# The last share of an output projection, its norm and the MLP's first tiles by halves of the tokens

## The chip, the cores and the metric

The kernel runs on one core of one Trainium2 chip, in one launch. The metric is the device time of the program in microseconds, the median of several runs. The engines that matter here are TensorE (PE, with its weight load PEld), VectorE (DVE), ScalarE (ACT), and SyncE (SP), which issues most DMAs.

## The reference

Two layers of a hybrid backbone for 512 latent tokens and 256 context tokens of width 1024. Cut to what matters:

```python
for l in range(2):
    need_ctx = l < 1
    hl = modulate(rmsnorm(xl, norm1[l]), ml[:, 0], ml[:, 1])      # latents
    hc = modulate(rmsnorm(xc, norm1[l]), mc[:, 0], mc[:, 1])      # context
    # hl @ w_in, hc @ w_in; three head groups: DeltaNet (256 columns of the output),
    # windowed attention (512), HGRN2 (256); the latents read the context, too
    yl = concatenate([dn_l, sw_l, hg_l], -1) @ w_out[l]           # 512 x 1024
    xl = xl + ml[:, 2] * yl
    h = modulate(rmsnorm(xl, norm2[l]), ml[:, 3], ml[:, 4])
    xl = xl + ml[:, 5] * (square(relu(h @ w_ff1[l])) @ w_ff2[l])  # 1024 -> 4096 -> 1024
    if need_ctx: ...                                              # the same for xc
return rmsnorm(xl, norm_f)
```

`rmsnorm` needs a sum over the 1024 channels of each token, so nothing of `h` for a token exists before all eight column tiles of the projection have been added into `xl` for that token.

## The kernel before

Activations lie with the channels on the partitions: `seg.x[k]` is 128 channels x 512 tokens (256 for the context), k = 0 to 7. Products are made in three matmuls of a high and a low part each (`product_t`, L544): the weights of one column tile come as one piece (`piece`, L534), SP loads it into a stage, ACT casts it into the high part (L540) and VectorE subtracts that to get the low part (L541); then, for each of the 128-row tiles of the input, L554 to L556 issue high x high, high x low and low x high into one PSUM bank. Stages and split weights are rings of two buffers each:

```python
self.st = Ring(self, 2, 1024)
self.ev = Ring(self, 2, 512)
self.wh = Ring(self.wmem, 2, 1024)
self.wl = Ring(self.wmem, 2, 1024)
```

A ring gives its buffers out in the order of the program, so the third user of a ring waits for the first one's readers; `ev` holds the squares, the diagonal and the modulated tiles of the norm. PSUM banks go out the same way, by kind (`bank`, L327): kind "d" (products and, before, the MLP's norm) has banks 0 and 1, "dn" (`product_n`, L560, the first product of a projection) 0, 1, 3, 4, 5, 6, and "n" 4 to 7.

The norm is `rstd` (L617): ACT squares each tile (L627), VectorE adds (L628), PE sums over the partitions with a column of ones (L631), VectorE runs a chain of small instructions (L634, L515 to L520) for the reciprocal root, lays it on a diagonal (L638), and PE spreads it over all partitions (L640). `modulated` (L643) then makes the eight input tiles: VectorE multiplies (L650), ACT adds the shift into the high part (L653), VectorE makes the low part (L654).

`out_proj` (L1464) makes the output projection for some of the eight input tiles ("yd" two, "ys" four, "yh" two), one column tile m after the other, each added into `seg.x[m]` (L1480). In layer 0 the latents' projection takes all eight input tiles at once; the program then has the MLP's norm and operand, then the next layer's projection of the context (`context_in`: four 800-wide pieces of `product_n`, nine products of 256 columns), then the context's own chain with the latents' MLP (L1486) as filling. In layer 1 the projection goes in three shares, "ys", "yh" and, last, "yd", whose pieces are 128 KB; then the two memory regions `r2` and `r3` change their type and the MLP and the final norm follow.

The order of instructions on each engine is set by a planner at build time, which runs the program through a model of its timing. It takes the ready instruction of the highest priority; priority is the order of the program, moved by `high_priority(500)` for everything in `piece` and by `ahead` for whole streams. On the chip each engine then runs its list in that order.

Of the kernel before, what the change touches and what calls it, by code (L numbers as in the profile page):

```python
# [19 lines left out]
DEPTH = 2  # L20
# [152 lines left out]
class Mem:  # L173
# [5 lines left out]
    def __init__(self, tile_ap, n):  # L179
        self.ap, self.n = tile_ap, n  # L180
        self.t = [0] * n
# [27 lines left out]
class Buf:  # L209
# [5 lines left out]
    def free(self):  # L215
        m = self.mem
        Mem.clock += 1
        m.t[self.i:self.i + self.nb] = [Mem.clock] * self.nb
        self.v = None


class Ring:
# [11 lines left out]
    def free(self):  # L234
        for b in self.b:
            b.free()


class Seg:
# [5 lines left out]
class Split:  # L245
# [59 lines left out]
class Net:  # L305
# [225 lines left out]
            yield c  # L531


    def piece(self, src, n=1024):  # L534
        nc = self.nc
        with self.tc.high_priority(500):
            st = self.st(n)
            nc.sync.dma_start(out=st, in_=src)
            hi, lo = self.wh(n), self.wl(n)
            nc.scalar.copy(hi, st)  # L540
            nc.vector.tensor_tensor(out=lo, in0=st, in1=hi.bitcast(F32), op=ALU.subtract)  # L541
        return hi, lo
# [75 lines left out]
    def rstd(self, seg, bk="d"):  # L618

        nc, T, nb = self.nc, seg.T, seg.nb  # L620
        acc = self.get(T, True)
        for k in range(8):
            if k == 0:
                nc.scalar.activation(out=acc.v, in_=seg.x[k], func=AF.Square)
            else:
                q = self.ev(T)
                nc.scalar.activation(out=q, in_=seg.x[k], func=AF.Square)  # L627
                nc.vector.tensor_tensor(out=acc.v, in0=acc.v, in1=q, op=ALU.add)  # L628
        ps = self.bank(bk)
        for b in range(nb):  # L630
            nc.tensor.matmul(ps[:, b:b + 1], lhsT=acc.v[:, b * 128:b * 128 + 128], rhs=self.c["ones"][:, 0:1], start=True, stop=True)  # L631
        acc.free()
        ms = self.small(nb)
        nc.vector.tensor_scalar(out=ms, in0=ps[:, :nb], scalar1=1.0 / D, scalar2=EPS, op0=ALU.mult, op1=ALU.add)  # L634
        rs = self.rsqrt(ms, nb)
        dg = self.ev(T)
        for b in range(nb):
            nc.vector.tensor_scalar(out=dg[:, b * 128:b * 128 + 128], in0=self.ident, scalar1=rs[:, b:b + 1], scalar2=None, op0=ALU.mult)  # L638
        pb = self.bank(bk)[:, :T]
        nc.tensor.matmul(pb, lhsT=self.c["ones"], rhs=dg, start=True, stop=True)  # L640
        return pb

    def modulated(self, l, which, seg, pb=None):  # L643
        nc = self.nc
        if pb is None:
            pb = self.rstd(seg)
        h = self.split(seg)
        for k in range(8):
            t = self.ev(seg.T)
            nc.vector.scalar_tensor_tensor(out=t, in0=seg.x[k], scalar=self.gmul[l][:, which, k, seg.idx:seg.idx + 1], in1=pb,  # L650
                                           op0=ALU.mult, op1=ALU.mult)
            sh = self.mod(l, 3 * which, k, seg)
            nc.scalar.activation(out=h.hi(k), in_=t, func=AF.Identity, bias=sh)  # L653
            nc.vector.scalar_tensor_tensor(out=h.lo(k), in0=t, scalar=sh, in1=h.hi(k).bitcast(F32), op0=ALU.add, op1=ALU.subtract)  # L654
        return h


    def in_piece(self, l, name):
# [802 lines left out]

    Y_TILES = {"yd": (0, 1), "ys": (2, 3, 4, 5), "yh": (6, 7)}

    def out_proj(self, l, seg, names=("yd", "ys", "yh"), mems=None):  # L1464

        nc, r = self.nc, seg.r
        ks = [k for n in names for k in self.Y_TILES[n]]
        y = [r[n][i] if n == "ys" else r[n][:, i] for n in names for i in range(len(self.Y_TILES[n]))]
        h = Split(mems or self.split_mems(), seg, len(ks))
        for k in range(len(ks)):  # L1470
            nc.scalar.copy(h.hi(k), y[k])
            nc.vector.tensor_tensor(out=h.lo(k), in0=y[k], in1=h.hi(k).bitcast(F32), op=ALU.subtract)
        for n in names:
            for b in ("sq0", "sq1") if n == "ys" else (n,):
                seg.b[b].free()
        if seg.x is None:
            self.x_load(seg)
        for m in range(8):
            def evac(seg, ps):
                nc.vector.scalar_tensor_tensor(out=seg.x[m], in0=ps, scalar=self.mod(l, 2, m, seg), in1=seg.x[m], op0=ALU.mult, op1=ALU.add)  # L1480
            yield from self.product_t(self.io["wout"][l, m][:, ks[0] * 128:(ks[-1] + 1) * 128], [(seg, h)], evac, len(ks))
        h.free()

    def mlp(self, l, seg):
        nc = self.nc
        h = self.modulated(l, 1, seg)  # L1486
        yield 0.0
        f = self.split(seg)
        for g in range(4):
            for k in range(8):  # L1490
                def evac(seg, ps):
                    t = self.ev(seg.T)
                    nc.scalar.activation(out=t, in_=ps, func=AF.Relu)  # L1493
                    nc.scalar.activation(out=t, in_=t, func=AF.Square)  # L1494
                    nc.scalar.copy(f.hi(k), t)  # L1495
                    nc.vector.tensor_tensor(out=f.lo(k), in0=t, in1=f.hi(k).bitcast(F32), op=ALU.subtract)  # L1496
                yield from self.product_t(self.io["ff1"][l, g * 8 + k], [(seg, h)], evac)
# [22 lines left out]
    def run(self, stop=None):  # L1520
        self.setup()
        lat, ctx = self.lat, self.ctx
# [58 lines left out]
        self.region_type(F32R, "r2", "r3")  # L1581
        run(bg.rest())
        self.project(1, (ctx,))
        run(self.out_proj(0, lat))
        mlp = self.mlp(0, lat)
        next(mlp)
        run(context_in())
        Ub = self.delta_open((ctx,))
# [46 lines left out]
        Ub.free()  # L1635
        self.region_type(F32R, "r1")
        run(self.out_proj(1, lat, ("yh",)))
        run(self.out_proj(1, lat, ("yd",)))
        self.region_type(F32R, "r2", "r3")
        run(self.mlp(1, lat))  # L1640
        self.finish()
        for n in ("r1", "r3", "r2"):
# [27 lines left out]
```

## Time and profile before

| | us |
|---|---|
| median of 3 runs | 2105.99 (2104.21 to 2106.32) |
| profiled execution, its own time | 2100.87 |
| its span | 2099.0 |
| PE, DVE, ACT busy | 1972.9, 1216.8, 858.1 |
| mean granted TensorE clock | 0.966 of full |

The span is what lies between the first and the last instruction of the profiled execution; busy times are sums of instruction durations and overlap. TensorE's clock has two levels, 1.0 and 0.5 of full speed in the rows. A matmul's row shows its whole passage, so the pace of a dense stretch is read from the starts of its rows, not from their durations.

### The profile page before, as it was taken

To read this page: it belongs to the slowest core of one execution; us is meant where nothing else is said; L and a number is where in the kernel's file an instruction comes from. 1 tells how busy PE (TensorE), PEld (TensorE's weight loads), DVE (VectorE), ACT (ScalarE), POOL (GpSimd) and SP (SyncE) were. 2 spreads that over 40 slices of the span, in tenths; PEclk is the share of its full clock that TensorE was granted. 3 is DMA by queue.
4 is the path that set the end of the run, shared out by engine and by line. 5 is a ranking of instruction groups with operands and counts; after the bars stand their busy time and mean duration, and the time that the engine had idled before them with its cause. 6 is when DMAs were issued, how large, how long until landed. Compare 5 with 4: busy or idle time off the path is not lost.

```text
span 2099.0 us, 37907 instructions
## 1 busy us (share of the span) xinstructions
PE 1972.9 (94%) x15456; PEld 1622.8 (77%) x15456; DVE 1216.8 (58%) x2737; ACT 858.1 (41%) x1703; POOL 143.7 (7%) x281
## 2 busy tenths in 40 slices
PE   5999999999999998799999998999889979999996
PEld 2787889879899997788788876767678747888884
DVE  4574883856976676766333334757787573333334
ACT  2432353335556663552524332425644234334241
POOL 0001333000000000011000000011200000000000
PEclk9999997999999999899999998999999989999998
DMA  8435343164232342333222246363300222222221
GB/s 341 155 111 166 99 121 112 42 237 152 100 112 102 102 160 72 129 127 119 81 91 100 90 151 192 114 208 121 111 2 13 72 70 101 91 101 91 100 91 70
DMA packets 72445, 242.43 MB, mean 115 GB/s; under 512 B 10192, under 2 KB 12368, under 8 KB 72144
## 3 DMA queue, kind: packets, MB, share of 16 engines
q1 hardware_dynamic: 57456, 197.35, 27.9%
q0 software_dynamic: 11792, 34.14, 5.1%
q10 hardware_dynamic: 3024, 8.53, 1.2%
q8 instruction: 121, 1.98, 0.4%
q14 instruction: 52, 0.43, 0.1%
HBM read 218.21 MB, written 19.14 MB: 113 GB/s over the span
## 4 chain that ended last, share of the span: by engine, by line
PE 80%; DVE 7%; DMA 5%; issue 4%; ACT 2%; POOL 1%; ACTq 0%; DVEq 0%; POOLq 0%; SPq 0%
PE psum L554 20%; PE psum L556 20%; PE psum L555 20%; PE psum L590 2%; PE psum L1452 2%; PE psum L1443 2%; PE psum L1390 1%; DMA arena<-in_ada 1%; PE psum L1117 1%; DVE weights L541 1%; PE psum L1075 1%; PE psum L1079 1%; DMA r<-in_ada 1%; DVE arena L1273 1%; DVE arena L1280 1%
## 5 line engine op out<-in xcount | busy, mean ns | idle before, releaser
L554 PE MATMUL psum<-r,weights 128*128 128x512 f32 (+1 forms) x2304 | 829.9, 361 | 11.0 <-ACT arena L725 3.8
L556 PE MATMUL psum<-r,weights 128*128 128x512 f32 (+1 forms) x2304 | 826.2, 360 | 2.1 <-DVE weights L541 2.0
L555 PE MATMUL psum<-r,weights 128*128 128x512 f32 (+1 forms) x2304 | 824.8, 358 | 0.4 <-DVE r L654 0.2
L540 ACT CAST weights<-arena 128x1024 fp32r<-128x1024 f32 (+3 forms) x295 | 293.7, 996 | 689.5 <-PE psum L555 601.2
L541 DVE TENSOR_TENSOR weights<-arena,weights 128x1024 fp32r<-128x1024 f32 (+3 forms) x295 | 340.8, 1156 | 298.0 <-ACT weights L540 289.4
L554 PEld LDWEIGHTS psum<-r,weights 128*128 128x128 f32 x2304 | 435.6, 189 | 95.5 <-issue 11.1
L556 PEld LDWEIGHTS psum<-r,weights 128*128 128x128 f32 x2304 | 435.6, 189 | 73.8 <-DVE weights L541 6.1
L555 PEld LDWEIGHTS psum<-r,weights 128*128 128x128 f32 x2304 | 435.9, 189 | 68.5 <-issue 3.0
L1500 DVE SCALAR_TENSOR_TENSOR arena<-psum,arena 128x512 f32<-128x512 f32 (+1 forms) x96 | 63.4, 661 | 196.8 <-PE psum L556 196.5
L1496 DVE TENSOR_TENSOR r<-arena,r 128x512 fp32r<-128x512 f32 (+1 forms) x96 | 57.4, 601 | 38.0 <-ACT r L1495 37.7
L653 ACT ACTIVATE r<-arena 128x512 fp32r<-128x512 f32 (+1 forms) x56 | 33.1, 628 | 71.3 <-DVE arena L650 71.3
L590 PE MATMUL psum<-arena 128*32 128x256 f32 x576 | 51.4, 406 | 9.3 <-DMA arena<-in_ada 8.7
L1494 ACT ACTIVATE arena<-arena 128x512 f32<-128x512 f32 (+1 forms) x96 | 54.1, 564 | 2.4
L1495 ACT CAST r<-arena 128x512 fp32r<-128x512 f32 (+1 forms) x96 | 52.8, 553 | 2.4
L1390 PE MATMUL psum<-r 128*128 128x256 f32 (+1 forms) x256 | 52.7, 321 | 0.5 <-ACT r L1423 0.5
L1493 ACT ACTIVATE arena<-psum 128x512 f32<-128x512 f32 (+1 forms) x96 | 50.2, 523 | 0.0
L1480 DVE SCALAR_TENSOR_TENSOR arena<-psum,arena 128x512 f32<-128x512 f32 (+1 forms) x40 | 27.7, 696 | 35.1 <-PE psum L556 34.8
L572 PE MATMUL psum<-weights,r 128*128 128x400 f32 x96 | 35.0, 378 | 10.7 <-DVE arena L650 10.1
L590 PE MATMUL psum<-r,arena 128*32 128x256 f32 x192 | 23.1, 497 | 19.2 <-DMA r<-in_ada 19.2
L1452 PE MATMUL psum<-arena 128*64 128x128 f32 x456 | 38.7, 294 | 2.2 <-ACT arena L1436 2.2
L650 DVE SCALAR_TENSOR_TENSOR arena<-arena,psum 128x512 f32<-128x512 f32 (+1 forms) x56 | 33.0, 628 | 12.9 <-PE psum L640 12.8
L1448 ACT COPY arena<-psum 128x512 f32<-128x512 f32 x53 | 31.1, 589 | 22.2 <-PE psum L1443 20.8
(426 smaller groups left out, 2573.5 us busy)
## 6 DMA issues: line engine op xcount, KB each, us to landing
arena<-in_ff SPq DMA_DIRECT2D x192, 512.0 KB, 3.2
arena<-in_ada SPq DMA_DIRECT2D x72, 512.0 KB, 4.9
arena<-in_win SPq DMA_DIRECT2D x51, 512.0 KB, 3.9
r<-in_ada SPq DMA_DIRECT2D x24, 512.0 KB, 5.4
arena<-in_wout SPq DMA_DIRECT2D x16, 512.0 KB, 3.6
arena<-in_win SPq DMA_DIRECT2D x12, 400.0 KB, 3.7
arena<-in_x ACTq DMA_DIRECT2D x8, 512.0 KB, 7.0
arena<-arena POOLq DMA_DIRECT2D x40, 64.0 KB, 4.6
```

The lines of the kernel that those rows point to most:

```text
L540: nc.scalar.copy(hi, st)
L541: nc.vector.tensor_tensor(out=lo, in0=st, in1=hi.bitcast(F32), op=ALU.subtract)
L554: nc.tensor.matmul(o, lhsT=hi[:, w], rhs=h.hi(k), start=k == 0, stop=False)
L555: nc.tensor.matmul(o, lhsT=hi[:, w], rhs=h.lo(k), start=False, stop=False)
L556: nc.tensor.matmul(o, lhsT=lo[:, w], rhs=h.hi(k), start=False, stop=k == nk - 1)
L590: nc.tensor.matmul(ps[32 * j:32 * j + 32, f * 256:f * 256 + 256], lhsT=self.csil[:, k, :], rhs=st[:, j * 256:j * 256 + 256], start=k == 0, ...
L1390: nc.tensor.matmul(o, lhsT=qs[:, kv], rhs=ks[:, kv, a, c0:c1], start=a == 0, stop=a == 1 and not more)
L1452: nc.tensor.matmul(py[heads[kv]], lhsT=self.vS[:, blocks[k0 + kt], heads[kv]], rhs=PT[:, c:c + 128], start=k0 + kt == 0, stop=k0 + kt == n ...
L1494: nc.scalar.activation(out=t, in_=t, func=AF.Square)
L1495: nc.scalar.copy(f.hi(k), t)
L1496: nc.vector.tensor_tensor(out=f.lo(k), in0=t, in1=f.hi(k).bitcast(F32), op=ALU.subtract)
L1500: nc.vector.scalar_tensor_tensor(out=seg.x[m], in0=ps, scalar=self.mod(l, 5, m, seg), in1=seg.x[m], op0=ALU.mult, op1=ALU.add)
```

## The change

The last share of the latents' output projection (layer 0: "yh", split off from the rest; layer 1: "yd") loads its weights as two pieces of four column tiles each and goes over the tokens in two halves of 256: for each half all eight column tiles, with the squares and their sum beside them, then that half's norm (its two banks now of kind "n"). Then both halves are modulated. In layer 1 the first two column tiles of the MLP go together, by halves. Other products are as before.

```diff
-    def piece(self, src, n=1024):
+    def piece(self, src, n=1024, parts=1):
...
-            nc.sync.dma_start(out=st, in_=src)
+            nc.sync.dma_start(out=st.rearrange("p (m c) -> p m c", m=parts) if parts > 1 else st, in_=src)
...
+    def token_rstd(self, acc, T, bk):       # the norm from the sum of squares on, for T tokens
...
+    def modulate(self, l, which, seg, h, ts, pb):   # the three instructions per k, on tokens ts
...
-    def out_proj(self, l, seg, names=("yd", "ys", "yh"), mems=None):
+    def out_proj(self, l, seg, names=("yd", "ys", "yh"), mems=None, last=None):
...
+        if last:
+            yield from self.last_share(l, seg, h, ks, last)
+            return
...
+    HALVES = slice(0, 256), slice(256, 512)
+
+    def last_share(self, l, seg, h, ks, mem_types):
+
+        nc = self.nc
+        w4 = [self.piece(self.io["wout"][l, m0:m0 + 4, :, ks[0] * 128:(ks[-1] + 1) * 128].rearrange("m p c -> p m c"), 1024, 4) for m0 in (0, 4)]
+        mem_types()
+        acc = self.get(512, True)
+        pbs = []
+        for ts in self.HALVES:
+            for m in range(8):
+                hi, lo = w4[m // 4]
+                o = self.bank("d")[:, :256]
+                for k in range(2):
+                    w = slice(m % 4 * 256 + k * 128, m % 4 * 256 + k * 128 + 128)
+                    nc.tensor.matmul(o, lhsT=hi[:, w], rhs=h.hi(k)[:, ts], start=k == 0, stop=False)
+                    nc.tensor.matmul(o, lhsT=hi[:, w], rhs=h.lo(k)[:, ts], start=False, stop=False)
+                    nc.tensor.matmul(o, lhsT=lo[:, w], rhs=h.hi(k)[:, ts], start=False, stop=k == 1)
+                x = seg.x[m][:, ts]
+                nc.vector.scalar_tensor_tensor(out=x, in0=o, scalar=self.mod(l, 2, m, seg), in1=x, op0=ALU.mult, op1=ALU.add)
+                q = self.ev(256) if m else acc.v[:, ts]
+                nc.scalar.activation(out=q, in_=x, func=AF.Square)
+                if m:
+                    nc.vector.tensor_tensor(out=acc.v[:, ts], in0=acc.v[:, ts], in1=q, op=ALU.add)
+            pbs.append(self.token_rstd(acc.v[:, ts], 256, "n"))
+            yield 8.0
+        acc.free()
+        seg.hm = self.split(seg)
+        for ts, pb in zip(self.HALVES, pbs):
+            self.modulate(l, 1, seg, seg.hm, ts, pb)
+        h.free()
+
+    def first_pair(self, l, seg, h, evacs):
+
+        nc = self.nc
+        ws = [self.piece(self.io["ff1"][l, k]) for k in range(2)]
+        os = [self.bank("d") for _ in ws]
+        for ts in self.HALVES:
+            for k in range(8):
+                w = slice(k * 128, k * 128 + 128)
+                for (hi, lo), o in zip(ws, os):
+                    nc.tensor.matmul(o[:, ts], lhsT=hi[:, w], rhs=h.hi(k)[:, ts], start=k == 0, stop=False)
+                    nc.tensor.matmul(o[:, ts], lhsT=lo[:, w], rhs=h.hi(k)[:, ts], start=False, stop=False)
+                    nc.tensor.matmul(o[:, ts], lhsT=hi[:, w], rhs=h.lo(k)[:, ts], start=False, stop=k == 7)
+        for o, evac in zip(os, evacs):
+            evac(seg, o)
+        yield 10.0
...
     def mlp(self, l, seg):
-        h = self.modulated(l, 1, seg)
+        pair = seg is self.lat and l == DEPTH - 1
+        h = seg.hm if seg is self.lat else self.modulated(l, 1, seg)
...
+            first = pair and g == 0
+            if first:
+                yield from self.first_pair(l, seg, h, [squared(0), squared(1)])
+            for k in range(2 if first else 0, 8):
+                yield from self.product_t(self.io["ff1"][l, g * 8 + k], [(seg, h)], squared(k))
...
-        run(self.out_proj(0, lat))
+        run(self.out_proj(0, lat, ("yd", "ys")))
+        run(self.out_proj(0, lat, ("yh",), None, lambda: None))
...
-        run(self.out_proj(1, lat, ("yd",)))
-        self.region_type(F32R, "r2", "r3")
+        run(self.out_proj(1, lat, ("yd",), [self.region["r1"][1]], lambda: self.region_type(F32R, "r2", "r3")))
```

## Rows read from the trace of the kernel before

**Rows 1.** The page, part 4: the chain that ended last, by engine.

```profile
PE 80%; DVE 7%; DMA 5%; issue 4%; ACT 2%; POOL 1%; ACTq 0%; DVEq 0%; POOLq 0%; SPq 0%
```

**Rows 2.** Waits of PE, whole run: us in total, times, longest us.

```profile
PE psum L631 <- DVE arena L628: 14.8, 6, 3.9
```

**Rows 3.** Windows: span, us, engines' busy (instructions), PEclk, DMA share, GB/s.

```profile
826.40:858.80 32.40, 15.76 (x58) 13.76 (x58) 20.11 (x42) 10.51 (x16) 0.53 (x1) 0.74 0.15 46
1691.50:1705.00 13.50, 12.52 (x48) 8.07 (x48) 11.64 (x21) 6.64 (x14) 0.00 (x0) 1.00 0.30 100
1705.00:1717.40 12.40, 3.10 (x10) 1.47 (x10) 8.56 (x24) 3.50 (x6) 0.00 (x0) 0.68 0.38 126
1717.40:1733.80 16.40, 14.99 (x48) 10.15 (x48) 10.00 (x15) 6.20 (x10) 0.00 (x0) 0.82 0.00 0
```

**Rows 4.** Timeline of PE, layer 0: start us, us, instruction [idle before <-releaser].

```profile
821.97 0.40 PE L554 MATMUL psum<-r,weights 128*128 128x512 f32 x1
...
825.91 0.39 PE L556 MATMUL psum<-r,weights 128*128 128x512 f32 x1
...
846.36 0.70 PE L572 MATMUL psum<-weights,r 128*128 128x400 f32 x1 [10.08 <-DVE arena L650]
...
858.84 0.38 PE L554 MATMUL psum<-r,weights 128*128 128x256 f32 x1 [3.83 <-ACT arena L725]
```

**Rows 5.** Timeline of PE, layer 1.

```profile
1704.60 0.39 PE L556 MATMUL psum<-r,weights 128*128 128x512 f32 x1
...
1717.42 0.80 PE L554 MATMUL psum<-r,weights 128*128 128x512 f32 x1 [1.65 <-ACT r L653]
...
1732.79 0.40 PE L556 MATMUL psum<-r,weights 128*128 128x512 f32 x1
...
1734.69 0.50 PE L556 MATMUL psum<-r,weights 128*128 128x512 f32 x1
```

**Rows 6.** Timeline of PE, products of the context, 256 columns.

```profile
499.80 0.28 PE L555 MATMUL psum<-r,weights 128*128 128x256 f32 x1
...
504.84 0.28 PE L555 MATMUL psum<-r,weights 128*128 128x256 f32 x1
...
860.27 0.41 PE L554 MATMUL psum<-r,weights 128*128 128x256 f32 x1
...
860.91 0.41 PE L554 MATMUL psum<-r,weights 128*128 128x256 f32 x1
```

**Rows 7.** Timeline of DVE, both layers (x2: two merged).

```profile
801.43 0.87 DVE L650 SCALAR_TENSOR_TENSOR arena<-arena,psum 128x256 f32<-128x256 f32 x2
...
1710.34 0.15 DVE L634 TENSOR_SCALAR arena<-psum 128x4 f32<-128x4 f32 x1
...
1712.71 0.87 DVE L638 TENSOR_SCALAR arena<-arena 128x128 f32<-128x128 f32 x4
1715.82 1.41 DVE L650 SCALAR_TENSOR_TENSOR arena<-arena,psum 128x512 f32<-128x512 f32 x2 [2.23 <-PE psum L640]
...
1725.99 1.42 DVE L654 SCALAR_TENSOR_TENSOR r<-arena,r 128x512 fp32r<-128x512 f32 x2
```

**Rows 8.** Groups by line and shape: count | busy us, mean ns | idle before.

```profile
L541 DVE TENSOR_TENSOR weights<-arena,weights 128x1024 fp32r<-128x1024 f32 x259 | 316.8, 1224 | 284.2 <-ACT weights L540 275.8 <-PE psum L1443 1.3 <-PE psum L555 0.3
...
L628 DVE TENSOR_TENSOR arena<-arena 128x256 f32<-128x256 f32 x21 | 8.8, 421 | 3.4 <-ACT arena L627 2.8
...
L540 ACT CAST weights<-arena 128x1024 fp32r<-128x1024 f32 x259 | 272.0, 1051 | 627.8 <-PE psum L555 573.9 <-issue 11.5 <-DMA arena<-in_win 10.8
```

**Rows 9.** DMA issues: count, KB each, median us from issue to landing.

```profile
arena<-in_wout SPq DMA_DIRECT2D x16, 512.0 KB, 3.6
...
r<-hi_lat POOLq DMA_DIRECT2D x1, 512.0 KB, 4.4
```

**Rows 10.** Timeline of SP, layer 1.

```profile
1688.55 0.33 SPq L538 DMA_DIRECT2D arena<-in_wout  x1
```

**Rows 11.** Chain that ended last, layer 0: start us, us, what.

```profile
850.72 5.01 DMA arena<-in_win
```

More of the change, by code (lines that the diff above doesn't have):

```diff
@@ L236, in free, with __init__, hi, lo @@
             b.free()
+class Part:
+    def __init__(self, h, ts):
+        self.h, self.ts = h, ts
+    def hi(self, k):
+        return self.h.hi(k)[:, self.ts]
+    def lo(self, k):
+        return self.h.lo(k)[:, self.ts]
 class Seg:
@@ L628, in rstd @@
                 nc.vector.tensor_tensor(out=acc.v, in0=acc.v, in1=q, op=ALU.add)
+        pb = self.token_rstd(acc.v, T, bk)
+        acc.free()
+        return pb
+    def token_rstd(self, acc, T, bk):
+        nc, nb = self.nc, T // 128
         ps = self.bank(bk)
         for b in range(nb):
-            nc.tensor.matmul(ps[:, b:b + 1], lhsT=acc.v[:, b * 128:b * 128 + 128], rhs=self.c["ones"][:, 0:1], start=True, stop=True)
-        acc.free()
+            nc.tensor.matmul(ps[:, b:b + 1], lhsT=acc[:, b * 128:b * 128 + 128], rhs=self.c["ones"][:, 0:1], start=True, stop=True)
         ms = self.small(nb)
@@ L647, in modulated @@
         h = self.split(seg)
+        self.modulate(l, which, seg, h, slice(0, seg.T), pb)
+        return h
+    def modulate(self, l, which, seg, h, ts, pb):
+        nc = self.nc
+        h = Part(h, ts)
         for k in range(8):
-            t = self.ev(seg.T)
-            nc.vector.scalar_tensor_tensor(out=t, in0=seg.x[k], scalar=self.gmul[l][:, which, k, seg.idx:seg.idx + 1], in1=pb,
+            t = self.ev(ts.stop - ts.start)
+            nc.vector.scalar_tensor_tensor(out=t, in0=seg.x[k][:, ts], scalar=self.gmul[l][:, which, k, seg.idx:seg.idx + 1], in1=pb,
                                            op0=ALU.mult, op1=ALU.mult)
@@ L654, in modulated @@
             nc.vector.scalar_tensor_tensor(out=h.lo(k), in0=t, scalar=sh, in1=h.hi(k).bitcast(F32), op0=ALU.add, op1=ALU.subtract)
-        return h
     def in_piece(self, l, name):
@@ L1482, in out_proj @@
         h.free()
+    HALVES = slice(0, 256), slice(256, 512)
[22 more added lines that the diff above has]
+            yield 8.0
+        acc.free()
+        seg.hm = self.split(seg)
+        for ts, pb in zip(self.HALVES, pbs):
+            self.modulate(l, 1, seg, seg.hm, ts, pb)
+        h.free()
@@ new lines, in first_pair @@
+    def first_pair(self, l, seg, h, evacs):
+        nc = self.nc
+        ws = [self.piece(self.io["ff1"][l, k]) for k in range(2)]
[10 more added lines that the diff above has]
+        yield 10.0
@@ L1489, in mlp, with squared @@
         for g in range(4):
-            for k in range(8):
+            def squared(k):
                 def evac(seg, ps):
@@ L1496, in evac @@
                     nc.vector.tensor_tensor(out=f.lo(k), in0=t, in1=f.hi(k).bitcast(F32), op=ALU.subtract)
-                yield from self.product_t(self.io["ff1"][l, g * 8 + k], [(seg, h)], evac)
+                return evac
+            first = pair and g == 0
[3 more added lines that the diff above has]
+                yield from self.product_t(self.io["ff1"][l, g * 8 + k], [(seg, h)], squared(k))
             for m in range(8):
```

## The prediction

> **What bounds the kernel now.** I read the page first, then the waits of PE, the stages by windows, the engines' timelines around the two places of the change, and the DMA rows. The chain that ended last is 80% matmul [rows 1], so time comes out of the whole only where TensorE stands still or runs at its low clock. The waits of PE over the whole run name the places: the norm's first matmul (L631, behind the sum of squares) [rows 2] and one wait of 10.1 us behind the modulation, L650 [rows 4]. The windows show what these cost around the change [rows 3]. In layer 0, from 826.4 to 858.8 us, PE is busy 15.8 of 32.4 us and the granted clock is 0.74. In layer 1, from 1705.0 to 1717.4, it is busy 3.1 of 12.4 us, and in the next 16.4 us, which hold the first two column tiles of the MLP, the clock is 0.82.
>
> Layer 0 in detail [rows 4]: the latents' output projection issues its last matmul at 825.91; the next layer's context projection follows in the program. Of its first product (four pieces, 48 matmuls of 400 columns) only the half for one token block runs on the first two pieces, and then PE stands until 846.36. Counting the calls of `bank`, the norm's broadcast lies in bank 1 (kind "d") and so does the second token block of that product (kind "dn"); the bank comes free only when the modulation has read the broadcast for the last time. Matmuls of the next products start at 858.84, 32.9 us after the projection's last. Layer 1 in detail [rows 5]: last matmul at 1704.60, first of the MLP 1717.42, the two tiles end with the one at 1732.79, and the third tile runs freely from 1734.69.
>
> **Prices.** A 512-column matmul takes 0.232 us at the full clock (17 steps from 821.97 to 825.91, rows 4). A 256-column one takes 0.120 us (42 steps from 499.80 to 504.84) and 0.21 us at the low clock (three steps from 860.27 to 860.91) [rows 6]. So a halved product costs 2 x 0.120 - 0.232 = 0.008 us more per pair: three places of 48 pairs, 1.2 us, and TensorE does not mind the halves. VectorE does: two modulation steps of 256 columns take 0.87 us, two of 512 take 1.41, so the pace is 0.39 against 0.67 [rows 7] and a cut instruction costs about 0.12 us more. An eviction I price like a modulation step, an add of squares at 0.34 (0.42 less an overlap of 0.08). Splitting a weight piece takes a cast of 1.05 us and a subtraction of 1.22 [rows 8]. The small chain of the norm runs from 1710.34 to 1712.71, 2.4 us, and each 128-column diagonal block 0.22 (0.87 for four): 2.8 us for a half [rows 7].
>
> **Layer 0, step by step.** (1) The first call now carries six of the eight input tiles: 48 matmuls of 512 fewer, 11.1 us, so it ends at about 815.0 instead of 826.1. Its 384 KB pieces are smaller than those before, hidden as they were. (2) The last share is 96 matmuls of 256, 11.5 us on PE. VectorE has in it 16 evictions (6.3), 14 adds (4.8), the subtraction of the second weight block (1.2), that of a context piece (1.0), and the whole chain of the first half (2.8): 16.1 us. VectorE is the longer one, and with two banks PE follows it: last add at about 832, 3 to 4 us later than before. (3) The broadcasts now lie in kind "n", banks 7 and 5 by the count of calls, and the context product in banks 0 and 1: the 10.1 us wait goes. What is late next is the supply of pieces. Two stages hold all pieces, and a transfer starts when the subtraction before it has emptied one: 5.0 us for the transfer [rows 11], then cast and subtraction, a round of 7.3. The rings of split weights are held by the two blocks of the share until its fourth and eighth tile of the second half, so the first context pieces are ready at about 829 and 832, the third and fourth a round later (839), and the fifth and sixth land at 841 to 844.5. The eviction of the 48 matmuls on ACT stands behind the casts that wait for these, as it does now. So the next products begin at about 846 instead of 858.84: 13 us. (4) VectorE has at 832 still the second chain, 32 modulation steps (12.6) and five subtractions (5.5): busy to about 853, and the convolutions of the context's first products queue behind. I take 2 us for it. Layer 0: 11 us less. Bounds: 16 if VectorE's 16.1 us ran at PE's 11.5; 4 if the products could go on only with VectorE free. The MLP's operand is then ready before 860 and first needed at about 875: hidden, and no cost.
>
> **Layer 1, step by step.** (1) The eight 128 KB pieces become two of 512 KB in 1 KB rows. SP's queue is as before up to there: the first is issued at 1688.55 [rows 10], when the ring of stages allows. No row shows this shape on this queue; the nearest are the 512 KB pieces of the same matrix in 4 KB rows (3.6) and a load of 512 KB in 1 KB rows by POOL (4.4) [rows 9], with 5.0 as the far end [rows 11]. I take 4.2, near the second because of the rows: landed 1692.8, split 1695.0. The ends are 1694.4 and 1695.8. PE, done with the share before at about 1691.4, waits 3 us here that it does not wait now. (2) From 1695.0 VectorE has one block's subtraction (1.2), 16 evictions (6.3), 14 adds (4.8), two chains (5.6), the subtractions of the MLP's first two pieces (2.4), and 32 modulation steps (12.6): 32.9 us. Without a hole it ends at 1727.9; now it ends at 1727.41 [rows 7]. The hole: `ev` has two buffers in the program's order, so the first half's second modulation step writes where the second half's diagonal lies until the second broadcast has read it. The early half can then use the wait of the late half through one buffer only. I take 1 us of holes: 1729. (3) The gain is behind that: now 24 matmuls of the second tile are left after the last modulation, since its bank held the broadcast; then six small ones are. PE has 96 matmuls of 256 from about 1717; at first at the low clock, as now to 1723 (26 at 0.21), then 70 at 0.120: 13.9 us, done at 1730 to 1731 against 1733.0. The third tile's wait for its weights and bank stays. Layer 1: 3 us less. Bounds: 6 less with the early landing and no hole; 4.5 more if all 96 run at the low clock (20.4 us from 1717).
>
> **Sum.** 11 + 3 = 14 us off the profiled execution's 2100.87 (span 2099.0 and 1.9 around it): 2086.9. The median of the runs is 5.1 us above that execution, and I carry the difference over: 2105.99 - 14 = 2092.
>
> [...]
>
> **Rivals.** *VectorE's queue takes layer 0 too* (0.20). The modulation of both halves stands ahead of the context's work and the products wait for it. For it: 16.1 us against 11.5 in the share, and 21 us of VectorE work from 832 on. Against: pieces have priority, and ACT, not VectorE, evicts the context's tiles. Layer 0 gains 6, layer 1 nothing: 2100.
>
> *VectorE starves TensorE and the clock goes with it* (0.12). Place: the last share of either layer and the pair of tiles. Where PE works 11.5 of 17 us the granted clock may fall to its lower level, as in the idle stretches [rows 3]. Price at the low clock: a share takes 96 x 0.213 = 20.4 us, 3 to 4 more than VectorE's, the pair the same: layer 1 ends at about 1742, 9 later; in layer 0 the pieces follow 4 us later and their 48 matmuls take 16 us instead of 9, which leaves 3 of the gain. Together 6 slower: 2112. It decides once the share takes more than about 19 us. Against it: in layer 1 the share before ran at clock 1.00 with PE busy 12.5 of 13.5 us.
>
> *Both waits go whole* (0.13). The planner fills VectorE's order well, so that the products begin at 842 and the pair ends at 1727: 17 + 6, 2083.
>
> *The gain is handed back* (0.05). The context's chain, which the latents' MLP only fills, ends when it did, and layer 1 stays: 2105.
>
> **How the numbers follow.** The forecast has 0.50, with a range of its own from 2087 to 2097. The range of 8 in 10 goes from 2083 (the third rival) to 2105 (the fourth); the slower case lies beyond. What this measurement can tell from no change is 0.2%, 4.2 us: faster is below 2101.8, which takes in the forecast, the third rival and two thirds of the first (0.13): 0.76. Within 0.2%: the rest of the first, the fourth, a little of the second: 0.13. Slower: 0.11.
>
> **What would show it.** Layer 0: no wait of L572 behind the modulation; the first product of 256 columns after the share at about 846; VectorE busy over 0.9 in the share and its last add near 832. Layer 1: the first block's transfer 3.6 to 5.0 us; a hole in PE of about 3 us before the share; the last modulation at 1727 to 1730 and the pair's end less than 2 us behind it, in that trace's time less layer 0's gain. I am wrong if the share takes PE's 11.5 us rather than VectorE's 16, if the clock in it is below 0.9, or if the products after it begin later than 852.

## The result and the profile after

The changed kernel is slower: 2117.48 us (median of 4 runs, 2116.32 to 2121.33) against 2106.15 for the kernel before beside it (4 runs), a ratio of 1.0061 with a 95% interval of [1.0044, 1.0079]. The forecast was 14 us faster; it is 11 us slower. The profiled execution took 2121.33 us, its span is 2119.5, the mean granted clock 0.959. Up to 480 us PE's instructions and their order are the same in both kernels, and yet the two profiled executions are already 3.4 us apart there. So below each place is measured from a mark beside it, not from the start of the span.

In the code after, the products are L567 to L569, the share L1526 to L1528 (eviction L1530, squares L1532, adds L1534), the ones matmul L651, the chain L653 and L528 to L533, the diagonal L657, the broadcast L659, the modulation L675, L678 and L679, the pair L1552 to L1554, and the evacuation (the copy out of PSUM) of the context product's v and i columns L749 (L725 before).

Waits of PE, whole run. Of before, [rows 2] shows the ones matmul's; the broadcast's was

```profile
PE psum L640 <- DVE arena L638: 10.6, 4, 4.3
```

After:

```profile
PE psum L659 <- DVE arena L657: 15.5, 6, 4.7
PE psum L651 <- DVE arena L641: 9.4, 4, 3.9
PE psum L651 <- DVE arena L1534: 7.9, 2, 4.3
PE psum L937 <- DVE arena L675: 6.1, 1, 6.1
PE psum L567 <- ACT arena L749: 5.1, 1, 5.1
```

The 10.1 us behind the bank [rows 4] are gone, as forecast. In their place stand waits for the second half's adds (L1534), more for the diagonals, and waits for the modulation (L675) and for an evacuation on ACT (L749). Windows (columns as in [rows 3]): layer 0's share and what follows it; layer 1's share, the rest of the norm, the pair of tiles.

```profile
817.60:831.90 14.30, 13.44 (x102) 12.38 (x100) 13.06 (x35) 6.93 (x14) 0.00 (x0) 1.00 0.23 67
831.90:868.70 36.80, 15.77 (x80) 14.40 (x80) 27.91 (x81) 17.48 (x36) 0.00 (x0) 0.65 0.22 72
1706.80:1723.00 16.20, 14.96 (x100) 13.61 (x100) 13.86 (x35) 6.57 (x14) 0.00 (x0) 0.89 0.23 75
1723.00:1735.50 12.50, 4.64 (x15) 3.08 (x14) 8.26 (x29) 3.63 (x7) 0.00 (x0) 0.67 0.22 80
1735.50:1752.10 16.60, 13.78 (x91) 13.03 (x90) 13.12 (x31) 8.42 (x18) 0.00 (x0) 0.83 0.00 1
```

VectorE does not slow layer 0's share so far that the clock falls: it is busy 13.06 of 14.3 us there, and the clock is 1.00. What is new is the long stretch behind it, in which PE is busy 15.8 of 36.8 us. PE's timeline there (of before: [rows 4]):

```profile
831.61 0.28 PE L1528 MATMUL psum<-r,weights 128*128 128x256 f32 x1
836.29 0.59 PE L659 MATMUL psum<-arena 128*128 128x256 f32 x2
845.61 1.01 PE L651 MATMUL psum<-arena 128*128 128x1 f32 x4 [4.34 <-DVE arena L1534]
851.28 1.19 PE L659 MATMUL psum<-arena 128*128 128x256 f32 x2 [4.66 <-DVE arena L657]
858.60 0.61 PE L937 MATMUL psum<-arena 128*64 128x16 f32 x8 [6.12 <-DVE arena L675]
868.72 0.58 PE L567 MATMUL psum<-r,weights 128*128 128x256 f32 x1 [5.12 <-ACT arena L749]
```

and ACT's, around the evacuation that PE waited for:

```profile
867.90 0.51 ACT L678 ACTIVATE r<-arena 128x256 fp32r<-128x256 f32 x1 [0.40 <-DVE arena L675]
868.32 0.35 ACT L749 COPY arena<-psum 128x256 f32<-128x256 f32 x1
```

The next products begin 37.1 us after the share's last matmul; before it was 32.9. Two things are seen. The second half's sum is ready only at 845.61, 14 us after its last matmul, though its evictions were done. And the v and i columns of the context product, whose last matmul starts at 840.92, are evacuated at 868.32, right behind the last modulated tile.

Layer 1, PE after (of before: [rows 5]):

```profile
1706.86 0.58 PE L1526 MATMUL psum<-r,weights 128*128 128x256 f32 x1 [2.05 <-ACT weights L553]
...
1725.85 0.67 PE L659 MATMUL psum<-arena 128*128 128x256 f32 x2 [2.76 <-DVE arena L657]
1730.07 1.01 PE L651 MATMUL psum<-arena 128*128 128x1 f32 x4 [3.54 <-DVE arena L1534]
1734.29 1.22 PE L659 MATMUL psum<-arena 128*128 128x256 f32 x2 [1.45 <-DVE arena L657]
1736.62 0.58 PE L1552 MATMUL psum<-r,weights 128*128 128x256 f32 x1 [1.12 <-ACT r L678]
1752.15 0.51 PE L567 MATMUL psum<-r,weights 128*128 128x512 f32 x1 [1.52 <-ACT arena L1569]
```

VectorE after, in the same place (of before: [rows 7]):

```profile
1725.23 0.48 DVE L657 TENSOR_SCALAR arena<-arena 128x128 f32<-128x128 f32 x2
1727.01 3.00 DVE L1534 TENSOR_TENSOR arena<-arena 128x256 f32<-128x256 f32 x6 [1.30 <-ACT arena L1532]
1730.11 0.48 DVE L675 SCALAR_TENSOR_TENSOR arena<-arena,psum 128x256 f32<-128x256 f32 x1
...
1735.55 0.87 DVE L675 SCALAR_TENSOR_TENSOR arena<-arena,psum 128x256 f32<-128x256 f32 x2 [1.32 <-PE psum L659]
1736.60 0.89 DVE L679 SCALAR_TENSOR_TENSOR r<-arena,r 128x256 fp32r<-128x256 f32 x2 [0.18 <-ACT r L678]
...
1749.59 0.48 DVE L679 SCALAR_TENSOR_TENSOR r<-arena,r 128x256 fp32r<-128x256 f32 x1 [0.58 <-ACT r L678]
```

Six of the second half's seven adds run in one block right after the first half's broadcast, and all but one of the sixteen modulated tiles after the second half's broadcast. The halves do not overlap: they run one behind the other. The prediction's sum for VectorE began when it had split the first weight block (here 1708.07) and ended with the last modulation (1750.07):

```profile
1708.07:1750.07 42.00, 31.60 (x199) 28.43 (x198) 33.53 (x93) 16.81 (x35) 0.00 (x0) 0.81 0.15 51
```

The work is as forecast, 33.5 us against 32.9, but it takes 42.0: 8.5 us of holes where the sum had 1. In e1 below, which has the same layer 1, it is 33.53 of 41.9 us.

The stretch from the last matmul of the share before to the third MLP tile splits so (us, from the starts of PE's rows in each kernel's one profiled execution; the rest is from there to the end of the span; e1 to e14 are the experiments below):

| | before | after | e1 | e8 | e9 | e4 | e10 | e13 | e14 |
|---|---|---|---|---|---|---|---|---|---|
| to the share's last matmul | 13.8 | 18.4 | 18.2 | 18.5 | 16.1 | 21.4 | 15.3 | 20.4 | 18.8 |
| to the last broadcast | 9.1 | 11.5 | 11.5 | 11.6 | 10.2 | 14.2 | 13.0 | 11.2 | 10.9 |
| to the third tile | 20.2 | 17.9 | 17.9 | 22.8 | 17.9 | 13.4 | 13.3 | 11.6 | 12.0 |
| whole stretch | 43.2 | 47.7 | 47.6 | 52.8 | 44.1 | 49.0 | 41.6 | 43.2 | 41.6 |
| the rest | 365.1 | 367.4 | 367.5 | 367.5 | 368.9 | 367.4 | 367.5 | 369.4 | 367.4 |

So layer 1 loses 4.5 us in the stretch and 2.3 us behind it. One execution can be some us off in the stretch: e3, whose layer 1 is the changed kernel's, has 49.4, and the experiments whose layer 1 is that of before have 42.3 to 42.8.

### The profile page after: what moved, and what is told of

Read it like the earlier page. It is cut to its first block, busy times and chain, and to the rows that moved or that the text cites. A ratio compares the mean times of both kernels' runs of the same rounds, so it can differ in the third digit from the quotient of the medians.

```text
span 2119.5 us, 38314 instructions
## 1 busy us (share of the span) xinstructions
PE 1986.5 (94%) x15604; PEld 1640.5 (77%) x15604; DVE 1232.5 (58%) x2827; ACT 864.8 (41%) x1731; POOL 144.2 (7%) x281
## 4 chain that ended last, share of the span: by engine, by line
PE 82%; DVE 9%; DMA 5%; ACT 2%; issue 2%; POOL 0%; ACTq 0%; DVEq 0%; POOLq 0%
PE psum L567 20%; PE psum L569 20%; PE psum L568 20%; PE psum L603 2%; PE psum L1476 2%; PE psum L1467 2%; PE psum L1414 2%; DMA arena<-in_ada 1%; PE psum L1141 1%; PE psum L1099 1%; PE psum L1103 1%; DVE weights L554 1%; DMA r<-in_ada 1%; DVE arena L1297 1%; DVE arena L1304 1%
## 5 line engine op out<-in xcount | busy, mean ns | idle before, releaser
L567 PE MATMUL psum<-r,weights 128*128 128x512 f32 (+1 forms) x2256 | 810.4, 360 | 9.1 <-ACT arena L749 5.1
L569 PE MATMUL psum<-r,weights 128*128 128x512 f32 (+1 forms) x2256 | 808.3, 359 | 0.9 <-DVE weights L554 0.8
L568 PE MATMUL psum<-r,weights 128*128 128x512 f32 (+1 forms) x2256 | 805.1, 357 | 0.1
L553 ACT CAST weights<-arena 128x1024 fp32r<-128x1024 f32 (+4 forms) x291 | 292.6, 1006 | 691.1 <-PE psum L568 597.4
L554 DVE TENSOR_TENSOR weights<-arena,weights 128x1024 fp32r<-128x1024 f32 (+4 forms) x291 | 340.1, 1169 | 298.3 <-ACT weights L553 289.6
L567 PEld LDWEIGHTS psum<-r,weights 128*128 128x128 f32 x2256 | 426.9, 189 | 89.2 <-issue 11.4
L569 PEld LDWEIGHTS psum<-r,weights 128*128 128x128 f32 x2256 | 426.2, 189 | 70.5 <-DVE weights L554 4.0
L568 PEld LDWEIGHTS psum<-r,weights 128*128 128x128 f32 x2256 | 426.5, 189 | 65.8 <-issue 2.4
L1582 DVE SCALAR_TENSOR_TENSOR arena<-psum,arena 128x512 f32<-128x512 f32 (+1 forms) x96 | 63.4, 661 | 202.4 <-PE psum L569 202.0
L678 ACT ACTIVATE r<-arena 128x256 fp32r<-128x256 f32 (+1 forms) x72 | 37.4, 552 | 74.6 <-DVE arena L675 74.5
L603 PE MATMUL psum<-arena 128*32 128x256 f32 x576 | 51.6, 415 | 11.1 <-DMA arena<-in_ada 10.6
L1571 ACT CAST r<-arena 128x512 fp32r<-128x512 f32 (+1 forms) x96 | 52.8, 553 | 2.4
L675 DVE SCALAR_TENSOR_TENSOR arena<-arena,psum 128x256 f32<-128x256 f32 (+1 forms) x72 | 36.3, 535 | 13.6 <-PE psum L659 13.2
L603 PE MATMUL psum<-r,arena 128*32 128x256 f32 x192 | 23.5, 503 | 20.4 <-DMA r<-in_ada 20.4
L1414 PEld LDWEIGHTS psum<-r 128*128 128x128 f32 x256 | 39.1, 204 | 3.1 <-ACT r L1447 1.6
L679 DVE SCALAR_TENSOR_TENSOR r<-arena,r 128x256 fp32r<-128x256 f32 (+1 forms) x72 | 36.8, 541 | 6.7 <-ACT r L678 5.8
L1476 PE MATMUL psum<-arena 128*64 128x128 f32 x456 | 37.1, 291 | 3.6 <-ACT arena L1460 3.6
```

The lines of the kernel that those rows point to most:

```text
L567: nc.tensor.matmul(o, lhsT=hi[:, w], rhs=h.hi(k), start=k == 0, stop=False)
L568: nc.tensor.matmul(o, lhsT=hi[:, w], rhs=h.lo(k), start=False, stop=False)
L569: nc.tensor.matmul(o, lhsT=lo[:, w], rhs=h.hi(k), start=False, stop=k == nk - 1)
L603: nc.tensor.matmul(ps[32 * j:32 * j + 32, f * 256:f * 256 + 256], lhsT=self.csil[:, k, :], rhs=st[:, j * 256:j * 256 + 256], start=k == 0, ...
L1414: nc.tensor.matmul(o, lhsT=qs[:, kv], rhs=ks[:, kv, a, c0:c1], start=a == 0, stop=a == 1 and not more)
L1476: nc.tensor.matmul(py[heads[kv]], lhsT=self.vS[:, blocks[k0 + kt], heads[kv]], rhs=PT[:, c:c + 128], start=k0 + kt == 0, stop=k0 + kt == n ...
```

## The experiments

Each kernel was timed against the kernel before on the same chip; the ratio is to that kernel. The chips differ between experiments, so ratios are compared, not microseconds.

**Each layer alone (e1, e2).** e1 keeps the old code in layer 0, e2 in layer 1:

```
-        run(self.out_proj(0, lat, ("yd", "ys")))
-        run(self.out_proj(0, lat, ("yh",), None, lambda: None))
+        run(self.out_proj(0, lat))                          # e1
...
-        run(self.out_proj(1, lat, ("yd",), [self.region["r1"][1]], ...))
+        run(self.out_proj(1, lat, ("yd",)))                 # e2, and pair = False
```

> Layer 0 as in the kernel before, layer 1 as in the changed one. Ring theory (the norm's two buffers, given out in the program's order, hold the second half's squares behind the first half's broadcast and the modulation behind the second one's): the layer-1 stretch from the end of the share before to the third MLP tile is 47.5 us as in the changed kernel against 42.5, so +5 us on the kernel before: 2111. Rival (VectorE's extra instructions only: 31 at 0.12 us and one more chain of 2.4): +6, 2112, with VectorE without holes between the share and the last modulation. If layer 0 alone carries the loss: 2106.

> Layer 0 as in the changed kernel, layer 1 as in the kernel before. The traces have the context products starting later by 5 to 6 us in layer 0, so both theories say 2111 to 2113; if the loss comes from layer 1 alone 2106, and 2117 if it all lies here.

e1: 2112.69 us, 1.0036 [1.0022, 1.0050]. e2: 2108.00, 1.0013 [1.0000, 1.0026]. That is 7.6 and 2.7 us; together 0.49% of the 0.61%, within the intervals. Neither layer has the forecast gain. For e1 the two theories lie too close to be told apart by time; the rival asked for a VectorE without holes, and there are 8.4 us of them. e2 lost less than the 5 to 7 us expected.

**The two work tiles (e3, e4).** `ev` has two buffers, given out in the order of the program: squares of the first half, its diagonal, squares of the second half, its diagonal, modulated tiles, then the evacuated v and i columns. e3 gives the latter two buffers of their own; e4 gives the whole last share (squares, diagonals, modulation) a ring of eight.

```
# e3
+        vt = Ring(self, 2, 256) if l == 1 and segs[0] is self.ctx else self.ev
-            t = self.ev(256)
+            t = vt(256)
# e4
+        ev, self.ev = self.ev, Ring(self, 8, 256)           # around last_share
```

> The changed kernel; only the two tiles that take the context product's last 256 columns get buffers of their own instead of the norm's ring. Ring theory: their copies on ACT no longer stand behind the last modulation, the wait of 5 us in front of the first 256-column product goes with the 20 us of idle PE before it, that product starts near 847 instead of 868.7 in the trace's time, and the run comes to 2098 (2094 to 2104). Rival (VectorE is full with the modulation of halves and nothing else can move): the first product moves by less than 5 us and the run stays within 4 us of the changed kernel, 2114 to 2118. Layer 1 is the same by either.

> The changed kernel; the last share, its norm and its modulation use a ring of eight buffers of 256 columns of their own in both layers, the old ring is left to the rest. Ring theory: layer 0 as with the tiles' own buffers (20 us less) and in layer 1 the second half's squares follow their evictions and the first half's modulation starts before the second broadcast: 6 to 9 us less there, together 2090 (2085 to 2098). Rival (VectorE full): layer 1 gains under 2 us, 2098 if layer 0 moves, 2116 if not.

e3: 2116.59 us, 1.0054 [1.0038, 1.0070]. e4: 2107.00, 1.0012 [1.0003, 1.0020]. e3's context products began 10.6 us after the share instead of 37.1, as expected, and yet it gained nothing that can be told: its time is the rival's, though not by the rival's mechanism. The reason is on PE's timeline of e3 (the share's last matmul is at 837.22):

```profile
847.84 0.38 PE L567 MATMUL psum<-r,weights 128*128 128x256 f32 x1 [0.97 <-ACT arena L752]
...
872.63 0.59 PE L659 MATMUL psum<-arena 128*128 128x256 f32 x2
881.82 0.62 PE L942 MATMUL psum<-arena 128*64 128x16 f32 x8 [8.36 <-DVE arena L675]
```

The second half's broadcast slips from 19.7 to 35.4 us after the share, and the hole comes there. e4 gives back 10 us, less than either expectation, and nothing in layer 1, whose stretch is 49.0. There the share ends 3 us later than in the changed kernel; behind it, the first half's modulation comes in between the instructions of the second half's chain, and the second broadcast stands on PE behind matmuls of the pair (second row of the table, 14.2). The third row gains 4.5, which does not make up for both.

**Is halving needed at all (e5, e11), and layer 0 alone with more tiles (e6, e12).** e11 is the kernel before with only the kind of the bank of layer 0's norm changed; e5 has e3's two tiles too. e6 is layer 0 of e4 with layer 1 of before, e12 has e3's tiles as well.

```
-            pb = self.rstd(seg)
+            pb = self.rstd(seg, "n" if seg is self.lat and l == 0 else "d")   # e11, e5
```

> The kernel before; only the bank of layer 0's norm is of kind "n". Theory A (with the bank free the context's evacuation still waits behind the modulation, since it writes a work tile that comes after them in the ring): at most 2 us, 2102 to 2105. Theory B (the bank was the whole wait): as with the two own tiles, 2096 to 2099.

> The kernel before, nothing cut in halves; only the bank of layer 0's norm is of kind "n" and the v and i columns of the context product are evacuated into two tiles of their own. Theory A (the ties were the loss, the halves are not needed): the products of 256 columns begin 10 us or so earlier and, as VectorE has no cut instructions more, most of it is kept: 2097 to 2101 against 2104.8. Theory B (the idle only moves on to the next place, as it did with the own tiles and the halves together): 2103 to 2106.

> Layer 0 in halves with eight work tiles of 256 columns of its own, layer 1 as before. If the layers simply add: the kernel with eight tiles in both layers (2107.0) less layer 1's loss (7.9): 2099. By its own layer 0 stretch alone (2.5 us shorter than before): 2102. If the gain of layer 0 with eight tiles was a matter of layer 1's code around it: 2105 or more.

> Layer 0 in halves with eight work tiles and the two own tiles for the v and i columns, layer 1 as before. If the own tiles add their gain: 2095 to 2098. If eight tiles already free the evacuation and VectorE's load sets the rest: as without them, 2098 to 2100.

e11: 2104.24 us, 0.9991 [0.9978, 1.0004]. e5: 2098.52, 0.9967 [0.9953, 0.9982]. e6: 2099.54, 0.9976 [0.9964, 0.9988]. e12: 2098.34, 0.9965 [0.9952, 0.9978]. The bank alone is worth nothing that can be told: the products still begin 28.9 us after the projection (32.9 before). ACT's timeline of e11 shows why; L723 is the copy beside L725 that needs no work tile.

```profile
842.84 0.42 ACT L723 COPY arena<-psum 128x128 f32<-128x128 f32 x2
...
858.40 0.72 ACT L653 ACTIVATE r<-arena 128x512 fp32r<-128x512 f32 x1 [0.72 <-DVE arena L650]
859.06 0.37 ACT L725 COPY arena<-psum 128x256 f32<-128x256 f32 x1
```

The same product, whose first columns were copied at 842.84, gives its other columns away 16 us later, behind the last modulated tile. With bank and tiles both, the tokens whole (e5), the products begin 12.3 us after the projection (at 843.93), and 7 us come out, as theory A had it. The halves with eight tiles (e6, e12) reach the same and no more; e12 lies on the border of its two expectations.

**Layer 1: the pair, the adds, the early blocks (e7 to e10).**

```
# e7: e4, and the adds on GpSimd
-                    nc.vector.tensor_tensor(out=acc.v[:, ts], ...)
+                    nc.gpsimd.tensor_tensor(out=acc.v[:, ts], ...)
# e8: e1 without the pair
+        pair = False
# e9: e1, e10: e4; both weight blocks in buffers of their own, split before the share ahead
+        self.w4 = [(hi, lo), (hi, lo)]                      # loaded ahead of out_proj(1, lat, ("yh",))
```

> As the kernel with eight work tiles, and the 28 adds of the squares go from VectorE to GpSimd. Theory VectorE (its load sets the end of both stretches): 28 adds of 0.34 to 0.42 are 10 to 12 us less on VectorE, half of it lands: 2099 to 2103, layer 1's stretch from 48.7 to about 45. Theory order and clock (TensorE's order of the pair's matmuls and its low clock set layer 1): layer 1's stretch stays at 48 to 49 and the time at 2105 to 2108. If an add on GpSimd takes over 1 us, the half's seven adds come late instead: over 2108.

> Layer 0 as before; in layer 1 the last share and the norm go by halves, the first two column tiles of the MLP do not. Theory work tiles (all modulation runs behind the second broadcast anyway, so that the halves of the pair can hide nothing): within 2 us of the kernel with the pair, 2111 to 2114. Rival (the pair's order on TensorE is what costs): 2107 to 2109.

> Layer 0 as before, layer 1 as changed, but the two weight blocks of the last share have buffers of their own and are loaded and split before the share ahead of it. Theory A (late block and low clock cost layer 1 its 5 to 6 us of a longer share): TensorE goes on into the share without a hole, at the full clock, the share ends about 13 us after the one before instead of 18, and of the loss of 7.9 some 4 to 5 go: 2107 to 2109. Theory B (VectorE's chain and the two work tiles set the end, the share has room): the second broadcast comes no earlier, 2111 to 2114.

> The changed kernel with eight work tiles of its own in both layers' last share, and layer 1's two blocks early. If the three losses of layer 1 (block, tiles, chain) add: layer 1's stretch 48.7 becomes 42 to 44, the time 2107 less 5 to 6: 2100 to 2102. If the pair's order on TensorE sets the end (its first half runs ahead of the second broadcast at the low clock): the stretch stays over 46, 2104 to 2107.

e7: 2106.28 us, 1.0004 [0.9990, 1.0017], layer 1's stretch 49.1: moving the adds to GpSimd does not shorten it. That does not clear VectorE's load as a cause, since little of it went: VectorE is busy 32.4 us in the stretch against 34.4 in e4, where the 14 adds would be 4.8 by the prediction's price (why is told at the end). e8: 2117.58, 1.0067 [1.0050, 1.0084], a miss on both expectations: without the pair layer 1 loses 14 us instead of 7.6. So the pair helps by about 6, also where nearly all modulation lies behind the second broadcast; the table has it in the third row, 17.9 against 22.8.

e9: 2112.64, 1.0036 [1.0021, 1.0051], no faster than e1, though its share ended 16.1 us after the one ahead of it instead of 18.2 and the stretch was 44.1. Most of the gain was spent earlier: the two subtractions now stand on VectorE ahead of the last head's norm, and PE waits for that longer.

```profile
1679.87 1.23 DVE L1727 TENSOR_TENSOR r<-arena,r 128x1024 fp32r<-128x1024 f32 x1 [0.37 <-ACT r L1726]
...
1681.20 1.23 DVE L1727 TENSOR_TENSOR r<-arena,r 128x1024 fp32r<-128x1024 f32 x1
```

```profile
1685.89 0.66 PE L1221 MATMUL psum<-arena,r 128*128 128x128 f32 x2 [6.64 <-DVE r L1213]
```

In e1 that wait is 3.96 us; another 1.4 us are lost in the rest (368.9 against 367.5). e10: 2103.48, 0.9993 [0.9978, 1.0008], against 1.0012 [1.0003, 1.0020] for e4. The stretch is 41.6 against 49.0, just below the 42 to 44 expected, but the intervals of the two times overlap, and the time is above the 2100 to 2102 expected. The wait ahead of the share is longer here, too (5.26 us, 3.96 in e4), which does not account for all of it.

**The diagonal (e13, e14).** One buffer for each half's diagonal instead of a work tile; e14 with e3's tiles too.

```
-        dg = self.ev(T)
+        dgb = self.get(T, True) if own else None     # own: in last_share
+        dg = dgb.v if own else self.ev(T)
```

> The changed kernel; only the diagonal of each half's norm lies in a buffer of its own instead of a work tile. Theory A (the diagonal is what ties the halves: the second half's squares and the first half's modulation wait for a broadcast): in each layer the second half's adds follow their evictions at once, the second broadcast comes some 4 us earlier and the first half's modulation no longer waits for it: 2107 to 2111 against 2117. Theory B (two work tiles for 256 columns are too few in any case, modulation at 0.93 us a half tile): 2113 to 2117.

> The same, and the v and i columns of the context product in two tiles of their own. If the diagonal and the context's evacuation together are what the eight work tiles gave in layer 0: 2105 to 2109. If the squares and the modulation themselves want more than two tiles: 2111 to 2116.

e13: 2107.29 us, 1.0004 [0.9987, 1.0020]. e14: 2097.76, 0.9967 [0.9954, 0.9980]. The one buffer gives back 0.57%, 12 us; the two tiles, worth nothing that can be told by themselves (e3), give 8 more on top of it. e13 came out as theory A had it, e14 better than both of its expectations. Layer 1 of e13, VectorE: the second half's adds follow their evictions, and the first half's modulation starts before the second diagonal (L658 here) is laid.

```profile
1716.17 0.42 DVE L1537 TENSOR_TENSOR arena<-arena 128x256 f32<-128x256 f32 x1
...
1718.69 0.87 DVE L678 SCALAR_TENSOR_TENSOR arena<-arena,psum 128x256 f32<-128x256 f32 x2 [0.45 <-PE psum L660]
...
1722.99 0.48 DVE L658 TENSOR_SCALAR arena<-arena 128x128 f32<-128x128 f32 x2
```

One part of theory A failed: the second broadcast comes no earlier, 11.2 us after the share's last matmul against 11.5. The gain lies behind it, where less modulation is left (11.6 us to the third tile against 17.9).

In layer 0 the evacuation of e13 still comes late; in e14 it comes early. PE's first product of the context in e13 and in e14:

```profile
863.83 0.58 PE L567 MATMUL psum<-r,weights 128*128 128x256 f32 x1 [5.00 <-ACT arena L752]
```

```profile
846.62 0.43 PE L567 MATMUL psum<-r,weights 128*128 128x256 f32 x1 [2.94 <-ACT arena L755]
```

That is 12.8 us after the share's last matmul in e14, against 30.1 and, in the changed kernel, 37.1.

Why 20 us less of this wait against before come out as 7 shows in the windows of 20 us from the share's end on. Kernel before, then e14:

```profile
825.90:845.90 20.00, 7.68 (x24) 5.99 (x22) 14.51 (x33) 5.37 (x9) 0.53 (x1) 0.66 0.07 21
845.90:865.90 20.00, 15.52 (x86) 14.67 (x87) 8.59 (x18) 10.66 (x18) 1.09 (x2) 0.83 0.36 119
865.90:885.90 20.00, 18.95 (x159) 18.55 (x158) 18.75 (x54) 8.92 (x18) 2.01 (x7) 1.00 0.43 145
```

```profile
833.80:853.80 20.00, 17.06 (x103) 16.62 (x102) 15.97 (x52) 12.29 (x23) 1.62 (x3) 0.91 0.48 156
853.80:873.80 20.00, 14.83 (x107) 14.51 (x106) 19.44 (x53) 10.09 (x22) 0.40 (x4) 0.75 0.32 106
873.80:893.80 20.00, 18.53 (x132) 17.30 (x131) 14.41 (x39) 9.10 (x17) 3.43 (x6) 0.99 0.54 171
```

PE stands 17.9 us in the three windows before and 9.6 in e14. The first window is filled; in the second VectorE is busy 19.44 of 20 us with modulation, subtractions and the context's convolutions, and PE waits there, 5.1 us at the longest. In e5 the second window has 19.94 of 20, and PE's longest wait is 8.1 us. From 40 us on both kernels are nearly whole again. So with and without halves VectorE is the engine that is full here; that it is the bound is read from the windows, and no run took load off it in this place without other changes.

## Why the prediction was wrong

The forecast was 11 us less in layer 0 and 3 in layer 1; alone, the layers came out 2.7 and 7.6 us slower (e2, e1). Two steps failed, and both overlooked what the ring `ev` ties together: layer 0, step (3), which put the evacuation behind the casts, and layer 1, step (2), which took 1 us of holes. With both ties taken out (e14) the kernel is 7 us faster, half of the forecast.

- *The bank wait goes.* Right: no wait of the context product behind the bank, its last matmul starts at 840.92 instead of 854.67.
- *The share at VectorE's pace, 16.1 us.* The price is about right: layer 0's share takes 14.0 us at clock 1.00, and six of its 14 adds, 2.0 us by the prediction's price, had moved behind it. The 16.0 in layer 1 agree in part by luck, since its first matmuls ran at the low clock (0.89 on average). VectorE was busy 0.91 of layer 0's share, as the sign asked. The last add near 832 was wrong: 845.
- *Layer 0, step (3): the next products at about 846.* This step failed: 868.72. The text put the evacuation on ACT "behind the casts that wait for these". It lies behind the modulation, because it writes a tile of `ev` that comes after all modulated tiles. Before, the last modulated tile was done 11 us ahead of it and the transfers came last, so the profile of before named only ACT [rows 4], and the tie could not be seen in it. With this tie and the diagonal's taken out, e14 has 846.62.
- *Layer 0, step (4): "I take 2 us" for VectorE's queue.* Too little. Through the diagonal the second half's sum was ready 14 us after its last matmul. Once that was mended (e14), the products began 20 us sooner behind the share than before, but PE's idle time in the 60 us from the share's end fell by 8 us only.
- *Layer 1, step (1): PE waits 3 us for the first block.* Right in kind: 2.05 us, and the matmuls behind it run at the low clock (0.21 us apart, until 1710.56). The share ended 4.6 us later after the one ahead of it than before.
- *Layer 1, step (2): "I take 1 us of holes" for `ev`.* This step failed: 8.5 us. The tie was named, and only one of its two ends was seen: not only does the first half's modulation wait for the second diagonal, the second half's squares wait for the first diagonal too, so that the halves follow one another. e13 against the changed kernel prices it, over both layers: 12 us; in layer 1 the stretch goes from 47.7 to 43.2, and 4.8 us of holes remain (VectorE busy 32.4 of 37.3 us).
- *Layer 1, step (3): the pair's early half is worth 3 us.* The mechanism is right where the tie is gone: in e14 the third part of the stretch is 12.0 against 20.2, and the whole, 41.6, is 1 us or so shorter than in the kernels with the old layer 1 (42.3 to 43.2). It is handed back behind it: with the same work, the rest took 2.3 us longer.
- *The rivals.* The outcome has the sign of the second (VectorE starves TensorE), but not its mechanism: the shares took 14 and 16 us, short of the 19 from which it was to decide. The place in layer 0 is the first rival's, though it saw a gain of 6 there. Its counterargument, that ACT evacuates the context's tiles, was what misled: which engine copies did not matter, the buffer did.
- *The cost of cut instructions.* The rows of the changed kernel have the price of before: a modulation step of 256 columns comes 0.39 us after the one ahead of it (L675: 0.87 for two, 0.48 for one), where one of 512 took 0.67 [rows 7], so about 0.12 us more for each cut. Layer 1's stretch has 5.6 us more of VectorE (30.4 to 36.0; 31 cut instructions and one more chain were put at 6). But e14 has the same cut instructions and no longer stretch than before: that cost is real and did not decide.

Open: why the MLP from the third tile on takes 2 us longer or more in all kernels with a halved layer 1 (the table's last row; 364.9 in e2, whose layer 1 is as before). Its 1498 matmuls come in the same order, and the clock is 1.00 in both in the windows compared, but a stretch of 40 us holds 174 to 175 of them where some of before hold 177 or 178. Whether the operands lie elsewhere in memory was not tested. In e9 and e13 the low clock still held for the first 3 to 5 us of it, which adds to their rest.

## What to carry to other kernels

Before work is cut in parts that are to overlap, list every buffer that the parts share, in the order in which the program takes it, and ask of each what its third user waits for: a wait that crosses from one part into the other turns the overlap into a queue. A tie that is hidden today, because another wait ends later, becomes the bound when that one goes (e11); the releaser that the profile of before named there was the last of several. And try the waits alone first: a bank of another kind and two own tiles, without any halves, gave here all that the halves gave at their best (e5 0.9967, e14 0.9967, e12 0.9965).

## What was not expected of the hardware

An add of 128 x 256 took 0.42 us on VectorE and 0.80 on GpSimd (e7, mean of 28), and some of VectorE's own instructions grew beside it. VectorE, then GpSimd, in layer 1 of e7:

```profile
1711.09 0.16 DVE L533 SCALAR_TENSOR_TENSOR arena<-arena 128x2 f32<-128x2 f32 x1
1711.28 0.58 DVE L531 SCALAR_TENSOR_TENSOR arena<-arena 128x2 f32<-128x2 f32 x1
...
1714.06 1.75 DVE L554 TENSOR_TENSOR weights<-arena,weights 128x1024 fp32r<-128x1024 f32 x1
```

```profile
1708.84 3.81 POOL L1535 TENSOR_TENSOR arena<-arena 128x256 f32<-128x256 f32 x4 [1.13 <-ACT arena L1533]
1713.21 1.52 POOL L1535 TENSOR_TENSOR arena<-arena 128x256 f32<-128x256 f32 x2 [0.56 <-ACT arena L1533]
```

Some instructions of 0.16 us take up to 0.58 here, the subtraction 1.75 instead of 1.22. The evictions, which read one operand from PSUM, kept their 0.48 us beside the adds. The two shown that grow read nothing from PSUM, and they grow by 0.42 and 0.53 us, less than one add on GpSimd; L533, which reads nothing from PSUM either, kept 0.16. What made the two grow, no run shows.
